# Hybrid decoder trunk on one core: activation sums of the down projection by accumulating transfers, two quadruples of weight blocks at a time, and an order of instructions set by other constants

## The chip, the cores and the metric

One of the eight cores of one Trainium2 chip runs the whole program in one launch. The metric is the device time of one execution in microseconds (us). Work is spread over the engines TensorE (PE, matrix products, with its weight loads PEld), VectorE (DVE), ScalarE (ACT), GpSimd (POOL) and SyncE (SP, which issues most transfers). Each engine takes its own instructions strictly in the order in which the program put them down, and waits on semaphores for those of other engines.

## The reference

A prompt of 1024 tokens and 8 samples of 8 tokens (1088 tokens together) go through one layer of width 1024. The part that the change is mostly about is the feed-forward part, with `D_FF = 2816`:

```python
x = x + mix @ lw['w_out']                       # mixer: attention, state space, pooling
hn2 = _rmsnorm(x, lw['norm2_g'])
up = hn2 @ lw['w_up']                           # 1024 -> 2 * 2816
up_c, conv_state = _causal_dwconv(up, conv_prefix, lw['conv_w'], lw['conv_b'])
a, g = jnp.split(up_c, 2, axis=-1)
x = x + (jax.nn.silu(g) * a) @ lw['w_down']     # 2816 -> 1024
y = _rmsnorm(x, norm_f_g)
```

Everything is float32; the mixer also returns keys, values and states.

## The kernel before

**Layout.** Features lie on the 128 partitions, tokens along the free dimension. A feature tile is [128, 1088]; `HT` = 544 is half of the tokens, `QT` = 272 a quarter. Each float32 product is made of three products of parts: an operand x is split into hi = round(x) (ACT cast to fp32r) and lo = x − hi (a TENSOR_TENSOR on DVE or POOL), and hi·hi, lo·hi, hi·lo are accumulated in PSUM.

**Order of the work.** `Driver` (line 185) steps Python generators by priority while the large products are put down; `Model` (line 36) keeps an estimate of when each engine is free, and a generator yields the estimated time at which its next step can run. So the order of instructions on each engine is fixed when the program is built, by the model's constants. Every engine call goes through one wrapper, so nearly every row of the profile bears line 156 (`L156`); instructions are told apart by the names of their tiles. `light(d)` (line 1607) gives a TENSOR_TENSOR to POOL if the model has POOL `d` us ahead of DVE, else to DVE; `parts` (line 1611) makes hi and lo, `sums` (line 1620) adds or subtracts two tiles.

**Mixer** (`phase_ab`, line 1224). The in-projection comes first, in `dense_group`s of 24 matmuls (`dps<-A,whl`). Beside it POOL computes the parameters of the state space part (`ssm_params`, line 476), ending with `ssm_cneg`, and `ssm_tables` (line 587) makes its tables; its six DVE operations `s_pn`, `X` read `ssm_pwp` and `ssm_cneg`. `bcast` (line 319) spreads 1/RMS over the partitions by a matmul of a broadcast column with the identity (`nbc`).

**Feed-forward, up** (`phase_c`, line 1625). Four feature tiles are made densely; while they run, DVE, POOL and ACT prepare the sums of the activations (`X<-X,X`, `T<-X,T`, `A<-X,A`, 128x544). Then 20 pairs f = 2 to 21 follow by `wino` (line 1575), Winograd's form of Strassen's scheme: seven products (op 0 to 6) of 24 matmuls of 272 columns on blocks of half the features and half the tokens, with PSUM tiles `wX`, `wY`, `wW`. Each result tile passes `conv` (line 1653; `cv<-raw`, 128x1104) and `gate` (line 1674; `th`), and each gated tile f goes to DRAM as `hs[f]`.

**Feed-forward, down.** Five blocks j of four feature tiles times four products mp give 20 products q = 4j + mp, each again seven ops of 12 matmuls (`wX<-hop,whl` and so on).
- Activations, per j: `hb` (line 1798) loads four tiles `hst<-hs`, makes the sums t1 to t4 (`tsums`: eight `hst<-hst` 128x544) and splits seven operands into `hop` (two halves of 544 each).
- Weights, per q: `draw` is loaded, `dsum` and `dw` (line 1856) make four sums of 128x256 (`wraw<-draw`, `draw<-...`) and seven splits `whl<-draw` / `whl<-wraw` of 128x256.
- Results: 14 additions `X<-wX,X` (`wY`, `wW`) of 128x272 from PSUM into the X tiles, on DVE.

A PSUM tile of a product comes from pools of 2, 5 and 1 banks (`bank`, line 1600) and is added to X piece by piece. The last pair of feature tiles is taken densely (`dn<-hl,whl`), followed by the norm (`final`, line 2039).

Of the kernel before, what the change touches and what calls it, by code (L numbers as in the profile page):

```python
# [12 lines left out]
P = 128  # L13
# [22 lines left out]
class Model:  # L36
    """Estimates when each instruction will run; the order in which the independent parts of the kernel
    are put down goes by it."""
    LAT = 0.13
    OWN = {"pe": 0.0, "dve": 0.1}  # L40

    def __init__(self):
        self.free = {}
        self.mem = {}
        self.ring = {}
        self.dma = 0.0
        self.tiled = False

# [9 lines left out]
    def ready(self, *aps, eng=None):  # L58
        """When the last writes to aps are done, as seen by an engine."""
# [26 lines left out]

    def note(self, eng, fn, args, kw):
# [9 lines left out]
        if fn == "dma_start":  # L97
            size = out.partition_size() * out.free_size() * 4
            self.free[eng] = start + (1.04 if eng == "pool" else 0.3)
            self.dma = max(self.dma, start + 1.4) + size / 360e3  # L100
            fin = self.dma + 1.7
        else:
            if eng == "pe":
                n = args[2].free_size()
                np_ = out.partition_size()
                if fn == "transpose":
                    c, np_ = 0.109, P
                elif args[1].dtype == F32R:
                    c = 0.0034 + n / 2400.0
                else:  # L110
                    c = 0.005 + max(4 * n / 2400.0, 0.213 * max(np_, 32) / 128.0)
                if np_ < P:
                    # column tiles run beside the first
# [3 lines left out]
                else:  # L117
                    c += 0.09 if self.tiled else 0.0
                    self.tiled = False
            elif eng == "dve":  # L120
# [8 lines left out]
            elif eng == "act":  # L129
                c = (0.07 if fn == "copy" else 0.12) + 0.83e-3 * n + (0.18 if len(outs) > 1 else 0.0)  # L130
            elif fn == "memset":
                c = 0.04 + 0.83e-3 * n
            else:
                c = 0.15 + (2.0e-3 if fn == "tensor_tensor" else 3.35e-3) * n
# [50 lines left out]
class Driver:  # L185
    """Steps the generators of the parts that run beside the large products.  A generator yields when
    its next step can run: a time, a condition, or None for at once."""
# [24 lines left out]
    def pick(self, t):  # L212
        """The generator to step: by priority among those ready at t, else the next to be ready."""
# [26 lines left out]
class Body:  # L240
# [8 lines left out]
    def acq(self, n):  # L249
        """Waits for n PSUM banks of the common ring."""  # L250
# [6 lines left out]
    def act(self, c, q, k):  # L257
        """The high (q = 0) or low part of feature tile k of the activations, token chunk c."""
# [9 lines left out]
    def rsqrt(self, x, n, width, pool=False):  # L268
        """x: [n, width] SBUF, overwritten; gives 1/sqrt(x).  pool: on Pool, else on DVE."""
# [49 lines left out]
    def bcast(self, c, y, bc=None):  # L319
        """y [tokens of a tile, tile] of chunk c as [128, tokens], the same on every partition."""  # L320
# [3 lines left out]
        for ti, (a, w) in enumerate(self.tok_tiles(c)):  # L324
            last = CH[c][1] == 320 and ti == 2
# [5 lines left out]
    def w_open(self, src, n, alloc=None):  # L331
        """src(i): DRAM AP [128, 4, 128] of half tile i; n: number of halves."""
# [40 lines left out]
    def w_split(self, upto):  # L373
        """Starts the splits of the product's halves before upto."""
# [6 lines left out]
    def dense_group(self, m, c, out_fn, last=True, pool=None):  # L381
        """One (feature tile, token chunk) of a product with K = 1024; last: the tile's last chunk."""
# [5 lines left out]
        for k in range(KD):  # L388
# [36 lines left out]
    def put_rms(self, c, y, own=False):  # L425
        """1 / RMS of chunk c to its place, the same on every partition."""
# [1783 lines left out]
```

## Time and profile before

| what | value |
|---|---|
| median of 3 runs | 1364.13 us |
| fastest and slowest run | 1362.97 and 1364.42 us |
| profiled execution, span from first to last instruction | 1362.6 us |
| median of the runs less this span | 1.5 us |
| mean granted clock of TensorE over the span | 0.970 |
| PE, DVE, POOL, ACT busy | 1272.4, 1031.8, 566.7, 539.4 us |

The span is that of one execution. The profile does not list its device time apart; what lies around the span (start and end of the launch) is taken as the 1.5 us between it and the median.
A row gives the start or a count, the busy time, engine, operation and tiles as output<-inputs. In square brackets stands how long the engine had been idle and the instruction that released it. [...]

### The profile page before, as it was taken

To read this page: it belongs to the slowest core of one execution; us is meant where nothing else is said; L and a number is where in the kernel's file an instruction comes from. 1 tells how busy PE (TensorE), PEld (TensorE's weight loads), DVE (VectorE), ACT (ScalarE), POOL (GpSimd) and SP (SyncE) were. 2 spreads that over 40 slices of the span, in tenths; PEclk is the share of its full clock that TensorE was granted. 3 is DMA by queue.
4 is the path that set the end of the run, shared out by engine and by line. 5 is a ranking of instruction groups with operands and counts; after the bars stand their busy time and mean duration, and the time that the engine had idled before them with its cause. 6 is when DMAs were issued, how large, how long until landed. Compare 5 with 4: busy or idle time off the path is not lost.

```text
span 1362.6 us, 26926 instructions
## 1 busy us (share of the span) xinstructions
PE 1272.4 (93%) x10466; PEld 1182.9 (87%) x10466; DVE 1031.8 (76%) x1990; ACT 539.4 (40%) x1127; POOL 566.7 (42%) x914
## 2 busy tenths in 40 slices
PE   7699899999999899978999999999999788888997
PEld 7697787777767899977999999999999688888997
DVE  5536765564378932897888888898889989999866
ACT  6222333333245422443545445455454333333333
POOL 7860430210012422593233232332335978768624
PEclk9899999999999999988999999999999889999997
DMA  9221212578874345202231221212212513222213
GB/s 339 87 81 33 68 40 83 183 240 289 281 246 149 83 138 157 65 24 102 106 112 55 88 82 62 95 65 79 95 49 99 186 56 113 97 68 91 81 44 132
DMA packets 80319, 154.84 MB, mean 114 GB/s; under 512 B 9856, under 2 KB 43136, under 8 KB 80192
## 3 DMA queue, kind: packets, MB, share of 16 engines
q1 hardware_dynamic: 78960, 149.68, 33.1%
q10 hardware_dynamic: 1152, 3.04, 0.6%
q8 instruction: 82, 1.34, 0.4%
q14 instruction: 45, 0.37, 0.1%
q0 software_dynamic: 80, 0.41, 0.1%
HBM read 124.04 MB, written 28.47 MB: 112 GB/s over the span
## 4 chain that ended last, share of the span: by engine, by line
PE 68%; DVE 18%; POOL 7%; issue 4%; DMA 1%; ACT 1%; POOLq 0%; DVEq 0%; SPq 0%; ACTq 0%
PE wX L156 23%; PE dps L156 15%; PE wY L156 11%; PE wW L156 5%; DVE X L156 5%; DVE whl L156 3%; POOL ssm_small L156 3%; DVE hop L156 2%; PE pv L156 2%; PE dn L156 2%; PE S L156 2%; DVE P L156 1%; PE yps L156 1%; PE od L156 1%; PE Sp L156 1%
## 5 line engine op out<-in xcount | busy, mean ns | idle before, releaser
L156 PE MATMUL dps<-A,whl 128*128 128x384 f32 (+1 forms) x1896 | 370.3, 344 | 29.7 <-DVE k L156 11.9
L156 PEld LDWEIGHTS dps<-A,whl 128*128 128x128 f32 x1896 | 319.9, 194 | 51.0 <-issue 14.9
L156 PE MATMUL wX<-T,whl 128*128 128x272 f32 x1440 | 193.0, 290 | 4.8 <-DVE whl L156 3.7
L156 PEld LDWEIGHTS wX<-T,whl 128*128 128x128 f32 x1440 | 186.1, 190 | 5.6 <-DVE whl L156 4.1
L156 PE MATMUL wX<-hop,whl 128*128 128x272 f32 x960 | 141.8, 300 | 27.1 <-DVE X L156 21.8
L156 PEld LDWEIGHTS wX<-hop,whl 128*128 128x128 f32 x960 | 130.8, 196 | 32.8 <-issue 12.1
L156 DVE SCALAR_TENSOR_TENSOR cv<-raw,vec,cv 128x1104 f32<-128x1104 f32 x88 | 126.0, 1431 | 12.2 <-ACT cv L156 10.8
L156 POOL TENSOR_TENSOR th<-th,cv 128x64 f32<-128x64 f32 (+1 forms) x40 | 79.8, 2013 | 131.2 <-DVE th L156 127.4
L156 PE MATMUL wY<-A,whl 128*128 128x272 f32 x960 | 127.6, 288 | 0.9 <-DVE whl L156 0.9
L156 PEld LDWEIGHTS wY<-A,whl 128*128 128x128 f32 x960 | 123.3, 188 | 1.1 <-DVE whl L156 1.1
L156 ACT CAST whl<-uraw 128x512 fp32r<-128x512 f32 x120 | 74.8, 623 | 81.0 <-PE wX L156 44.2
L156 ACT CAST whl<-draw 128x256 fp32r<-128x256 f32 (+1 forms) x122 | 47.8, 415 | 143.4 <-POOL draw L156 33.3
L156 POOL COPY cvo<-raw 128x2 f32<-128x2 f32 x88 | 27.6, 343 | 167.2 <-DVE raw L156 154.9
L156 ACT CAST whl<-wraw 128x512 fp32r<-128x512 f32 (+1 forms) x92 | 52.3, 570 | 112.4 <-PE dps L156 63.7
L156 DVE TENSOR_TENSOR whl<-uraw,whl 128x512 fp32r<-128x512 f32 x120 | 87.2, 727 | 12.5 <-ACT whl L156 9.9
L156 DVE TENSOR_TENSOR whl<-wraw,whl 128x512 fp32r<-128x512 f32 (+1 forms) x90 | 67.0, 745 | 31.2 <-ACT whl L156 31.2
L156 DVE TENSOR_TENSOR X<-wX,X 128x272 f32<-128x272 f32 x160 | 66.6, 431 | 14.3 <-PE wX L156 14.0
L156 PE MATMUL wY<-hop,whl 128*128 128x272 f32 x480 | 69.1, 293 | 1.0 <-DVE whl L156 1.0
L156 DVE TENSOR_TENSOR uraw<-uraw 128x512 f32<-128x512 f32 x40 | 69.2, 1729 | 0.7
L156 PEld LDWEIGHTS wY<-hop,whl 128*128 128x128 f32 x480 | 64.6, 193 | 1.6 <-DVE whl L156 1.6
L156 ACT ACTIVATE P<-P,sm 128x128 f32<-128x128 f32 (+7 forms) x64 | 35.7, 558 | 74.0 <-DVE sm L156 74.0
L156 PE MATMUL wW<-A,whl 128*128 128x272 f32 x480 | 63.2, 288 | 0.0
(271 smaller groups left out, 2336.1 us busy)
## 6 DMA issues: line engine op xcount, KB each, us to landing
K<-in_ck_dram SPq DMA_DIRECT2D x40, 512.0 KB, 6.3
V<-in_cv_dram SPq DMA_DIRECT2D x80, 256.0 KB, 4.4
uraw<-in_w_up_dram SPq DMA_DIRECT2D x40, 512.0 KB, 4.0
hs<-th SPq DMA_DIRECT2D x22, 544.0 KB, 2.7
hst<-hs SPq DMA_DIRECT2D x22, 544.0 KB, 5.3
draw<-in_w_down_dram SPq DMA_DIRECT2D x20, 512.0 KB, 3.5
wraw<-in_w_in_dram SPq DMA_DIRECT2D x28, 256.0 KB, 3.1
X<-xs SPq DMA_DIRECT2D x8, 544.0 KB, 4.4
```

Of the source, the lines that this page charges most:

```text
L156: return f(*args, **kw)
```

## The change

**Activations of the down projection.** `gate` stores its result with signs into a DRAM array per block (`hj[j]`, four blocks of two half tiles each) where before it stored whole tiles. The sums t1 to t4 are no longer computed by POOL or DVE: `chain` loads a block by SP and adds further blocks to it in SBUF with an accumulating transfer (`accum_op`) issued from POOL, 20 in all. The operand is split in the whole (128x1088) by ACT and DVE. Two chains run beside each other for each j, each in one buffer, each step waiting for the split of the step before. For j = 1 the second buffer is `T10`, apart from the gate's buffer `th`. The blocks' signs are such that sums suffice; the results of ops 1, 2 and 4 are subtracted from X, and op 3's weights are negated.

**Weights.** Two products q are handled as one pair p, so that sums and low parts are 512 wide (11 on DVE per p) instead of 256; none is on POOL. In the first pairs, where two tiles hold the draws, they are still 256 wide.

**Results.** PSUM is given anew for the down projection (`pq`, eight banks as two tags of two tiles of two banks), a product's two halves lie in one tile, and one addition of 544 follows where there were two of 272.

**Order.** `Model` gets other constants and a rule that DVE and POOL operations with two SBUF inputs exclude each other; `light` chooses POOL only if it is 2 us ahead; `parts` puts the low part always on DVE. The conv and gate of f = 21 (the last pair) come only after the first pair of weights. In the mixer, `ssm_tables` yields until `ssm_cneg` is ready, and `bcast` uses a transpose.

Counts of instructions that the order shows:

| | before | after |
|---|---|---|
| DVE, POOL, ACT instructions | 1992, 919, 1056 | 1913, 733, 987 |
| `hst<-hst` sums on POOL and DVE | 37 and 3 | none |
| accumulating transfers on POOL's queue | 0 | 20 |
| `hop` low parts | 70 of 544, 47 on DVE | 35 of 1088, all on DVE |
| weight sums and low parts of the 20 products on POOL | 118 | 0 |
| additions into X in the down projection | 280 of 272 | 140 of 544 |

The core of the diff:

```diff
-        yield None
+        yield self.M.ready(self.pwp, self.cneg)
...
-            nc.tensor.matmul(bc[:, a + (64 if last else 0):a + 128], y[:, ti:ti + 1].to_broadcast([P, 128]),
-                             self.ident[:, 64:128] if last else self.ident[:, :], start=True, stop=True)
+            nc.tensor.transpose(bc[:, a:a + 128], y[:, ti:ti + 1].to_broadcast([P, 128]), self.ident)
...
-        return self.nc.gpsimd if self.M.free.get("pool", 0.0) + d < self.M.free.get("dve", 0.0) else self.nc.vector
+        return self.nc.gpsimd if max(d, 2.0) < 9.0 and self.M.free.get("pool", 0.0) + 2.0 < self.M.free.get("dve", 0.0) else self.nc.vector
...
-            self.light(d).tensor_tensor(l, a, h.bitcast(F32), ALU.subtract)
+            yield max(self.M.ready(h), self.M.free["dve"] - 0.3 - late)
+            self.nc.vector.tensor_tensor(l, a, h.bitcast(F32), ALU.subtract)
...
-            yield lambda: n["ga"[m % 2]] >= m // 2
+            yield lambda: n["ga"[m % 2]] >= m // 2 and (m < 42 or n["dw"] >= 0)
...
-            nc.sync.dma_start(self.hs[f], th)
+            if f < 20:
+                b = f % 4 // 2 * 2
+                nc.sync.dma_start(self.hj[f // 4][:, b:b + 2, f % 2], th.rearrange("p (h t) -> p h t", h=2))
+            else:
+                nc.sync.dma_start(self.hs[f], th)
...
+        def chain(j, t, steps):
+            for pos, op, blk, add in steps:
+                yield max(M.avail(t, "dma"), M.ready(self.hj[j]))
+                if add:
+                    yield M.free["pool"] - 1.0
+                    g.dma_start(out=t, in_=self.hj[j][:, blk].rearrange("p k t -> p (k t)"), accum_op=ALU.add)
+                else:
+                    nc.sync.dma_start(t, self.hj[j][:, blk].rearrange("p k t -> p (k t)"))
+                if op is None:
+                    continue
+                yield M.ready(t)
...
+                hi, lo = [ring(j, 2 * pos + q, [P, 2, HT], F32R, "hop") for q in range(2)]
+                yield from self.parts([hi.rearrange("p k t -> p (k t)")], [lo.rearrange("p k t -> p (k t)")], [t], 9, 0 if j else 99)
...
+                    st = [cp.tile([P, NTOK], F32, tag="rms", name="hst", bufs=1),
+                          fp.tile([P, NTOK], F32, tag="T10" if j == 1 else "th", name="hst", bufs=1)]
...
+                D.add(chain(j, st[0], ((1, None, 0, False), (1, 4, 1, True), (2, 5, 3, True), (6, 3, 2, True))), "hb", 0.4)
+                D.add(chain(j, st[1], ((0, 0, 0, False), (3, 2, 3, False), (4, 6, 1, True), (5, 1, 2, False))), "hb", 0.3)
...
+        pq = self.psum_pool("pq", 2)
+        for p in range(10):
+            ps = {}
+            for op in (0, 4, 5, 2, 6, 1, 3):
...
+                    x = self.X[m][:, HT * h:HT * h + HT].rearrange("p (c t) -> p c t", c=2)
+                    v.tensor_tensor(x, x, o[:, :, :QT], ALU.subtract if op in (1, 2, 4) else ALU.add)
```

DVE in the mixer, before, from the low parts ahead of the state space tables on (`s_pn`, `X_92`: the tables; `k_671`: the key tile out of PSUM; `whl<-wraw,whl`: the low part of a weight):

```order
L156 TENSOR_TENSOR s_pn<-ssm_pwp,bc_in 128x512
L156 TENSOR_TENSOR X_92<-ssm_pwp,ssm_cneg 128x512
L156 TENSOR_TENSOR s_pn<-s_pn,X_92 128x512
L156 TENSOR_TENSOR s_pn<-ssm_pwp,ssm_cneg 128x512
L156 TENSOR_TENSOR X_92<-ssm_pwp,bc_in 128x512
L156 TENSOR_TENSOR whl<-wraw,whl 128x512
L156 TENSOR_TENSOR k_671<-dps,rms 128x384 x2
```

and in the changed kernel at the same place:

```order
L188 TENSOR_TENSOR whl<-wraw,whl 128x512
L188 TENSOR_TENSOR k_671<-dps,rms 128x384
L188 TENSOR_TENSOR s_pn<-ssm_pwp,bc_in 128x512
L188 TENSOR_TENSOR X_92<-ssm_pwp,ssm_cneg 128x512
L188 TENSOR_TENSOR s_pn<-s_pn,X_92 128x512
```

One weight's low part and the first key chunk now stand ahead of the tables; two key chunks stay behind them.

DVE in the middle of the down projection, before:

```order
L156 TENSOR_TENSOR X_11918<-wX,X_11918 128x272 x2
L156 TENSOR_TENSOR draw<-draw 128x256
L156 TENSOR_TENSOR hop<-hst,hop 128x544 x2
L156 TENSOR_TENSOR X_11920<-wY,X_11920 128x272 x2
L156 TENSOR_TENSOR X_11918<-wX,X_11918 128x272
L156 TENSOR_TENSOR whl<-draw,whl 128x256
```

and in the changed kernel:

```order
L188 TENSOR_TENSOR X_11602<-X_11602,wW 128x544
L188 TENSOR_TENSOR draw<-wraw,draw 128x2x256
L188 TENSOR_TENSOR hop<-hst,hop 128x1088
L188 TENSOR_TENSOR X_11604<-X_11604,wW 128x544
L188 TENSOR_TENSOR hop<-hst,hop 128x1088
L188 TENSOR_TENSOR X_11357<-X_11357,wX 128x544
L188 TENSOR_TENSOR whl<-wraw,whl 128x2x256
```

All pieces are twice as long, `hop` among them, and all of this work is on DVE. Nothing but transfers stands on POOL's queue in that stretch (`hj_104` to `hj_108` are the DRAM blocks j = 0 to 4):

```order
L188 DMA hst<-hj_105 128x1088 x3
L188 DMA hst<-hj_106 128x1088 x4
L188 DMA hst<-hj_107 128x1088 x4
L188 DMA hst<-hj_108 128x1088 x4
L188 DMA out_conv_dram<-cvo 128x792
L188 TENSOR_TENSOR wraw<-sqs 128x384
```

Before, this place held the 37 sums, 23 low parts of `hop` and the 118 weight operations.

DVE at the start of the feed-forward part, before (`X<-X,X` and `T<-X,T`: activation sums; the two `whl` rows: low parts for the dense tiles):

```order
L156 TENSOR_TENSOR X_88<-X_88 128x544
L156 TENSOR_TENSOR X_85<-X_89,X_85 128x544
L156 TENSOR_TENSOR whl<-wraw,whl 128x512
L156 TENSOR_TENSOR X_88<-X_92,X_88 128x544
L156 TENSOR_TENSOR X_87<-X_91,X_87 128x544
```

and in the changed kernel:

```order
L188 TENSOR_TENSOR X_86<-X_86 128x544
L188 TENSOR_TENSOR X_87<-X_87 128x544
L188 TENSOR_TENSOR X_88<-X_88 128x544
L188 TENSOR_TENSOR X_86<-X_90,X_86 128x544
L188 TENSOR_TENSOR X_87<-X_91,X_87 128x544
L188 TENSOR_TENSOR X_88<-X_92,X_88 128x544
L188 TENSOR_TENSOR X_89<-X_89,X_85 128x544
L188 TENSOR_TENSOR whl<-wraw,whl 128x512
```

Seven activation sums stand on DVE ahead of the first of these `whl` rows where there were two, and of 18 such sums that POOL had in this part, 14 are now DVE's.

## Rows read from the trace of the kernel before

**Rows 1.** The page's head, and busy time of each engine over the span.

```profile
span 1362.6 us, 26926 instructions
PE 1272.4 (93%) x10466; PEld 1182.9 (87%) x10466; DVE 1031.8 (76%) x1990; ACT 539.4 (40%) x1127; POOL 566.7 (42%) x914
```

**Rows 2.** Stretches: us, busy PE, PEld, DVE, ACT, POOL (count), clock, DMA share, GB/s.

```profile
50.00:69.00 19.00, 7.05 (x41) 6.73 (x39) 6.43 (x11) 0.00 (x0) 17.17 (x62) 0.79 0.28 87
...
573.00:655.00 82.00, 68.16 (x417) 66.76 (x416) 71.38 (x77) 34.98 (x68) 49.06 (x49) 0.90 0.20 70
655.00:1033.60 378.60, 378.60 (x3020) 378.60 (x3020) 332.53 (x450) 185.95 (x341) 114.00 (x180) 1.00 0.24 81
1033.60:1058.00 24.40, 21.86 (x170) 21.21 (x169) 24.30 (x27) 12.23 (x24) 16.84 (x13) 1.00 0.29 102
1058.00:1293.00 235.00, 206.92 (x1502) 200.36 (x1501) 218.03 (x396) 86.49 (x197) 183.89 (x168) 0.94 0.28 97
1293.00:1315.70 22.70, 22.70 (x182) 22.70 (x181) 16.79 (x37) 6.58 (x14) 8.36 (x12) 1.00 0.21 66
```

**Rows 3.** The waits of PE: tile, releaser: total us, times, longest.

```profile
PE wX L156 <- DVE X L156: 21.8, 15, 4.0
```

**Rows 4.** Timeline, 62 to 79 us, of the early stall.

```profile
63.43 0.69 DVE L156 TENSOR_TENSOR X<-ssm_pwp,ssm_cneg 128x512 f32<-128x512 f32 x1 [12.50 <-POOL ssm_cneg L156]
...
68.94 9.60 PE L156 MATMUL dps<-A,whl 128*128 128x320 f32 x42 [11.95 <-DVE k L156]
```

**Rows 5.** Timeline of PE from 548 to 646 us: a broadcast, dense groups, and stalls.

```profile
548.71 0.83 PE L156 MATMUL nbc<-ident,rs_y 128*128 128x128 f32 x6
...
573.34 17.46 PE L156 MATMUL dps<-A,whl 128*128 128x384 f32 x106
597.91 12.79 PE L156 MATMUL dps<-A,whl 128*128 128x384 f32 x60 [7.11 <-DVE whl L156]
...
616.66 11.48 PE L156 MATMUL dps<-A,whl 128*128 128x384 f32 x59 [3.00 <-DVE whl L156]
...
637.70 4.69 PE L156 MATMUL wX<-T,whl 128*128 128x272 f32 x23 [2.90 <-DVE whl L156]
642.22 3.19 PE L156 MATMUL wY<-A,whl 128*128 128x272 f32 x24
```

**Rows 6.** Timeline of POOL and DVE from 599 to 603 us.

```profile
599.68 1.83 POOL L156 TENSOR_TENSOR T<-X,T 128x544 fp32r<-128x544 f32 x1
...
602.59 0.71 DVE L156 TENSOR_TENSOR T<-X,T 128x544 fp32r<-128x544 f32 x1
```

**Rows 7.** Groups by form, 1037 to 1315 us: count | busy us, mean ns | idle before.

```profile
L156 DVE TENSOR_TENSOR X<-wX,X 128x272 f32<-128x272 f32 x158 | 65.8, 431 | 13.7 <-PE wX L156 13.4
L156 POOL TENSOR_TENSOR hst<-hst 128x544 f32<-128x544 f32 x37 | 60.8, 1661 | 3.9 <-DVE hop L156 3.3 <-DVE hst L156 0.7
L156 DVE TENSOR_TENSOR hop<-hst,hop 128x544 fp32r<-128x544 f32 x47 | 58.3, 1260 | 0.0
...
L156 ACT CAST hop<-hst 128x544 fp32r<-128x544 f32 x70 | 42.7, 644 | 31.2 <-POOL hst L156 20.4 <-DVE hst L156 10.8
```

**Rows 8.** Timeline of DVE from 1166 to 1168 us.

```profile
1166.39 0.71 DVE L156 TENSOR_TENSOR hop<-hst,hop 128x544 fp32r<-128x544 f32 x1
1167.02 0.43 DVE L156 TENSOR_TENSOR X<-wX,X 128x272 f32<-128x272 f32 x1
1167.37 0.42 DVE L156 TENSOR_TENSOR X<-wW,X 128x272 f32<-128x272 f32 x1
```

**Rows 9.** View of the tile whl on DVE: duration ns min/median/max, 512 wide.

```profile
L156 DVE TENSOR_TENSOR whl<-uraw,whl x120: 674/688/1835, 625.7 to 1051.1; 128x512 fp32r<-128x512 f32 x120
```

**Rows 10.** View of the tile hst: DVE's one low part 1088 wide, and its transfers' landing.

```profile
L156 DVE TENSOR_TENSOR hl<-hst,hl x1: 1274/1274/1274, 1279.9 to 1279.9; 128x1088 fp32r<-128x1088 f32 x1
...
DMA to landing us min/median/max: 3.4/5.3/8.0
```

**Rows 11.** View of the DMA issues: POOL's one transfer, KB and us to landing.

```profile
out_conv_dram<-cvo POOLq DMA_DIRECT2D x1, 396.0 KB, 5.8
```

More of the change, by code (lines that the diff above doesn't have):

```diff
@@ L47, in __init__, with clear @@
         self.tiled = False
+        self.port = {"dve": [], "pool": []}
+        self.win, self.act, self.slow = 0, 0.0, True
+    def clear(self, eng, t):
+        other = self.port["pool" if eng == "dve" else "dve"]
+        for a, b in reversed(other[-40:]):
+            if a <= t < b:
+                return self.clear(eng, b)
+        return t
     def seg(self, ap):
@@ L85, in alloc, with clock, two @@
         self.mem[name] = [t, {}, {}]
+    WIN = 4.096 / 1.2
+    def clock(self, t, c):
+        w = int(t / self.WIN)
+        while self.win < w:
+            self.slow = self.act < 0.42 * self.WIN
+            self.win, self.act = self.win + 1, 0.0
+        self.act += c
+        return 2 * c if self.slow else c
+    def two(self, args, kw):
+        x = [a for a in list(args[1:]) + [kw.get("in0"), kw.get("in1")] if hasattr(a, "bitcast") and a.free_size() > 1]
+        return all(a.space != bass.MemoryType.PSUM for a in x)
     def note(self, eng, fn, args, kw):
@@ L119, in note @@
                     self.tiled = False
+                c = self.clock(start, c)
             elif eng == "dve":
@@ L133, in note @@
             else:
-                c = 0.15 + (2.0e-3 if fn == "tensor_tensor" else 3.35e-3) * n
+                c = 0.13 + (2.6e-3 if fn == "tensor_tensor" else 3.35e-3) * n
+            if eng == "pool" and fn != "memset" or eng == "dve" and self.two(args, kw):
+                start = self.clear(eng, start)
+                self.port[eng].append((start, start + c))
             fin = start + c
@@ L1203, in run @@
             self.xs = [dram.tile([P, NTOK], F32, name="xs%d" % k) for k in range(8)]
-            self.hs = [dram.tile([P, NTOK], F32, name="hs%d" % f) for f in range(NFF)]
+            self.hj = [dram.tile([P, 4, 2, HT], F32, name="hj%d" % j) for j in range(5)]
+            self.hs = {f: dram.tile([P, NTOK], F32, name="hs%d" % f) for f in (20, 21)}
             self.wraw = self.wp.tile([P, 3, 4, 128], F32, name="wraw")
@@ L1897, in dw @@
-            for q in (20, 21):
-                yield lambda: n["down"] >= 4
-                r = draw.pop(q)
-                hi, lo = [ring(1, 2 * (q - 18) + z, [P, 4, 2, 128], F32R, "whl") for z in range(2)]
-                yield from self.parts([hi], [lo], [r])
-                dops[q] = (hi, lo)
-        n["dw"] = n["ds"] = n["s1"] = -1
-        def dsum():
-            for q in range(20):
-                yield lambda: q in draw and n["s1"] >= q - 2
-                a11, a12, a21, a22 = [draw[q][:, z] for z in range(4)]
-                yield M.ready(draw[q])
-                yield from self.sums(0, (s1s[q % 2], a21, a22, ALU.add), (a21, a11, a21, ALU.subtract))
-                n["ds"] = q
+            D.add(dsums(), "dsums", 0.6)
@@ L1913, in dw_1 @@
+            yield lambda: n["down"] >= 4
+            rs, qs, at = draw.pop(10)
+            for q in range(2):
+                hi, lo = [ring(1, 2 * (q + 2) + z, [P, 4, 2, 128], F32R, "whl") for z in range(2)]
+                yield from self.parts([hi], [lo], [rs[0][:, q]])
+                dops[20 + q] = (hi, lo)
+        n["dw"] = n["dw5"] = n["ds"] = -1
         def dw_1():
-            yield lambda: n["up"] == NFF or (n["up"] == NFF - 1 and n["pos"] >= 4)
+            yield lambda: n["up"] == NFF
@@ L1990, in out @@
                     if c == 1:
-                        fc[2 * f] = D.add(conv(2 * f), "conv", 3 if f < 21 else 2)
+                        fc[2 * f] = D.add(conv(2 * f), "conv", 3 if f < 20 else 4)
                 else:
@@ L1995, in out @@
                     if c == 1:
-                        fc[2 * f + 1] = D.add(conv(2 * f + 1), "conv", 3 if f < 21 else 2)
-                        fg[f] = D.add(gate(f), "gate", 1 if f < 20 else 2)
+                        fc[2 * f + 1] = D.add(conv(2 * f + 1), "conv", 3 if f < 20 else 4)
+                        fg[f] = D.add(gate(f), "gate", 1 if f < 20 else 4)
             def done(op):
@@ L2036, in phase_c @@
+        self.pt = self.psum_pool("pe", 8)
         g.dma_start(self.o["conv"], cvo)
@@ L2078, in phase_c @@
             ss = []
-            acc = fp.tile([P, 384], F32, tag="raw", name="acc", bufs=2)
+            acc = self.wr[0].rearrange("p a m -> p (a m)")[:, :384] if c % 2 else wr[:, 512:896]
             for m in range(8):
```

278 lines of the change are left out of this document (143 added, 135 removed).

## The prediction

> **What bounds the kernel now.** Start with the page's head and busy shares [rows 1]: TensorE is busy 1272.4 of 1362.6 us, so 90 us are left idle, and part of the busy time runs at a lowered clock. The question is where. The table of stretches [rows 2] answers it: from 655 to 1033.6 us (the up projection) PE is busy all the time at clock 1.00, 3020 matmuls in 378.6 us, 0.1254 us each. Nothing that another engine saves there can shorten the span. Three stretches are different: 50 to 69 us (PE busy 7 of 19), 573 to 655 us (68 of 82, clock 0.90), and the down projection from 1058 to 1293 us (207 of 235, clock 0.94). In the last 22.7 us of the down projection, where the weights are ahead, PE is full again: 182 matmuls, 0.125 us each.
>
> For the down projection, count from the first product of f = 21 to the first `dn`: 24.4 + 235.0 + 22.7 = 282.1 us [rows 2]. PE alone needs (168 + 20 x 84) x 0.1254 = 231.7 us. So 50 us are lost, the largest sum in the program. The waits of PE name the end of it: PE waits 15 times, 21.8 us together, for DVE's addition into X [rows 3]. DVE is busy 218 of 235 us there [rows 2], but not with work at full speed: its low parts of 544 take a mean of 1.260 us [rows 7], and the same form 0.71 us when alone [rows 8]. POOL, 184 us busy in the same stretch [rows 2], runs operations with two SBUF inputs, and where both engines do, they take turns: a sum of this size takes POOL 1.83 us and DVE, once POOL is done, 0.71 us [rows 6]. So DVE is late because of POOL, the bank is free late, PE stops, its clock falls.
>
> **The change, part by part.** The sum is made against the profiled execution, 1362.6 us, with 1.5 us around it, which gives the median, 1364.1.
>
> *Down projection, DVE.* POOL's 37 sums (60.8 us [rows 7]) and its low parts vanish, and nothing in this stretch competes with DVE. DVE's own price is read from starts, not durations: 0.63 us from a 544 to the next start, 0.35 us for a 272 [rows 8]: 0.07 us plus 1.03 ns an element. That gives 0.60 us for 512 and 1.19 us for 1088, where single rows show 0.688 [rows 9] and 1.274 [rows 10]. One pair p now costs 14 x 0.63 + 11 x 0.60 + 3.5 x 1.19 = 19.6 us of DVE (I use 20, with a little for small rows between). PE needs 168 x 0.1254 = 21.1 us. So PE is the bound in the middle six pairs and the last two, which lack some `hop`.
>
> The start is not covered: conv and gate of f = 21 are put behind the first weights, and there the pieces are still 256 wide. From the start of f = 21 through the second pair DVE has 28 additions (17.6), 44 pieces of 256 (15.0), 11 of 512 (6.6), 13 `hop` (15.5), eight conv passes of 1104 (9.7), the gates (4.6) and small ones (3): 72 us, against 3 x 21.1 = 63.3 of PE. So DVE is the bound there, by 9 us. Sum: 72 + 8 x 21.1 = 241. In-order waits come on top: DVE is as full as before (20 of 21.1 us, against 218 of 235), and that cost 28 us of idle PE [rows 2]. But an addition had some 1.5 us (one product of 12 matmuls) before its bank was wanted, and now has three of them. I take 8 of 28: 249 us. Ends: 239, nothing lost and a third of the 9 saved; 262, half of the old waits kept and the start late by 7 more. **Gain 33 us (20 to 43).**
>
> *Adding transfers.* No row shows a transfer that adds. The nearest: the same 544 KB loaded plainly, 5.3 us median and 3.4 to 8.0 [rows 10], and POOL's one transfer, 396 KB, 5.8 us [rows 11]. From below, 5.3; from above, twice the longest, 16 (read, add and write back). I take 7, close to the rows that exist. One chain has for each j a load, three adds of L us and three splits between: cast 2 x 0.644 less one start [rows 7], low part 1.27 [rows 10], and 0.5 of waits, 2.9 us. So 5.3 + 3L + 3 x 2.9 = 14 + 3L, and two pairs of PE are 42.1: the transfer is hidden up to L = 9.4. At 7 it costs nothing; that cover gone, each us costs three per j. The queue that carries it, POOL's, has nothing else in this stretch, so nothing stands behind its waits but the next adds.
>
> *Casts on ACT.* Same elements in half as many pieces; ACT is busy 86 of 235 us [rows 2]: nothing.
>
> *Start of the feed-forward part.* PE waits 7.11, 3.00 and 2.90 us for a low part [rows 5] (and 0.8 in two small ones), and runs slow after each: 60 matmuls in 12.79 us where 106 took 17.46 (0.165 each, 2.9 lost), 59 in 11.48 (1.8 lost), 23 in 4.69 against 24 in 3.19 (1.6 lost). Together 20 us. 14 of POOL's 18 sums become DVE's: 14 x 1.83 = 25.6 us of taking turns [rows 6] become 14 x 0.64 = 9. But DVE, in order, now has seven sums ahead of the first `whl`, so the 7.1 us wait stays; the later low parts stand some 6 us earlier, and those two waits and their slow matmuls mostly go. **Gain 8 (3 to 18).**
>
> *Early stall.* DVE sat 12.5 us behind `ssm_cneg`, with the key tile's evictions queued behind it, and PE 11.95 us behind those [rows 4]. Now one key chunk and one low part go ahead of the tables. That frees one bank: PE has 24 more matmuls, 24 x 9.60 / 42 = 5.5 us, before it stops for the second chunk, still behind the tables. POOL's own end does not move. **Gain 5 (0 to 10).**
>
> *Broadcasts.* 18 of six passes, 0.59 us each to the next start [rows 5], become 18 of three: at most half, 18 x 0.3 = 5. I take **2 (0 to 4)**. The rest of the mixer's order, and the last dense pair: 0, either way by 4.
>
> Sum: 33 + 8 + 5 + 2 = 48; 1364.1 - 48 = **1316 us**.
>
> **The rivals.** *A. DVE's operations don't overlap in time.* Then a pair costs 14 x 0.71 + 11 x 0.688 + 3.5 x 1.274 = 22.0 us, over PE's 21.1, in six pairs (5 more), and the first stretch grows by 120 x 0.07 = 8. The down projection takes 259, the gain is 23 + 15: **1326**. Against it: the addition at 1167.02 starts 0.63 us after the 544 piece that lasts 0.71 [rows 8]. For it: not every pair of pieces is ready back to back.
> [...]
>
> *B. The adds land later than the order assumes.* DVE takes its row in order, and a `hop` whose operand is not there holds the additions behind it, for which PE waits. If each of the 16 adds for j = 1 to 4 is 2 us late, 32 us of DVE stop; the pair's spare us (21.1 - 20) over eight pairs takes 9, and some overlap: 18 net. **1334**. For it: 5.3 varies up to 8.0 [rows 10].
>
> *C. Early gains don't come.* Waits in the mixer and at the start of the feed-forward part move on to the next late row (PE behind the second key chunk, DVE's longer queue ahead of `whl`), and the change does there nothing that it could: 1364 - 33 = **1331**. For it: total DVE work grows there, and POOL's end stays.
>
> *D. Slower: the adding transfer sets the pace.* The chain binds above L = 9.4; each us beyond costs 3 us in each of the four blocks j = 1 to 4, 12 us. The other gains are used up at L = 9.4 + 48/12 = 13.4. At L = 15, near the upper bound: 1316 + 12 x 5.6 = **1383**. For it: no row shows such a transfer, DVE is busy nearly all the time beside it, and a plain one reaches 8.0 [rows 10]. Against it: POOL's transfer landed in 5.8 us with DVE at work [rows 11].
> [...]
>
> **How the numbers follow.** Forecast 0.54, A 0.15, B 0.13, C 0.11, D 0.05, and 0.02 that losses eat all. 1316 is that of the likeliest. Its own range is 1299 to 1330 (all gains at their low ends give 1341, all at their high ends 1289). To hold A to C as well, with their own spread, the range reaches from 1296 to 1340. A measurement can tell about 0.2%, 2.7 us, from no change: faster 0.93 (all but D and the 0.02), same 0.02, slower 0.05.
>
> **What would show it.** Right: from the first product of f = 21 to the first `dn` 245 to 255 us, PE's wait for the addition into X under 10 us, 512-wide low parts in the down projection at 0.69 us and hardly ever over 1, adds landing in 6 to 8 us, `hop` not waited for by PE. In 573 to 655, two of the three waits gone. Wrong: additions into X waiting behind `hop` with `hop` waiting for a transfer (B, D); a median add over 9.4 us (D); DVE rows in the down projection starting only at the end of the row before (A).

## The result and the profile after

Median 1334.49 us over 4 runs (1332.78 to 1337.15), against 1364.01 of the kernel before: ratio 0.9784, 95% interval 0.9771 to 0.9798, faster by 2.2%. Forecast were 1316, range 1296 to 1340. The profiled execution took 1334.44 us, its span is 1332.3.

First the page's head and the busy times.

```profile
span 1332.3 us, 26297 instructions
PE 1258.9 (94%) x10412; PEld 1169.6 (88%) x10412; DVE 965.4 (72%) x1911; ACT 527.6 (40%) x1058; POOL 339.8 (26%) x728
```

POOL lost 227 us and DVE 66, yet the span lost 30 [rows 1]. Where, the stretches tell: early stall, end of the mixer, start of the feed-forward part, up projection, first two pairs of the down projection, the rest of it. Columns are those of [rows 2]; the clock is TensorE's granted one, a mean over the stretch, and the traces of both kernels record it as 1.00 or 0.50 and as nothing else.

```profile
50.00:69.00 19.00, 12.98 (x74) 12.24 (x72) 9.89 (x17) 1.61 (x3) 17.19 (x58) 0.90 0.38 117
440.00:490.00 50.00, 39.44 (x189) 35.87 (x188) 38.15 (x101) 15.20 (x37) 15.91 (x20) 0.80 0.24 52
581.50:625.40 43.90, 40.58 (x240) 39.97 (x239) 40.53 (x55) 21.97 (x43) 22.71 (x25) 0.97 0.13 43
625.40:1038.80 413.40, 404.24 (x3194) 402.34 (x3193) 330.50 (x502) 199.06 (x385) 113.15 (x189) 1.00 0.28 84
1060.20:1111.80 51.60, 43.88 (x314) 42.55 (x313) 47.83 (x81) 20.89 (x38) 6.70 (x9) 0.93 0.85 243
1111.80:1263.20 151.40, 150.61 (x1190) 149.68 (x1189) 141.94 (x204) 55.99 (x75) 10.94 (x13) 1.00 0.56 144
```

In the last row PE is full at clock 1.00 and POOL has nothing but its transfers, where before PE was 207 of 235 and POOL 184 [rows 2]. Read from PE's timeline, by four marks (last broadcast of the mixer, first product of f = 2, first product of f = 21, first `dn`), all in us:

| piece | before | after | difference | forecast |
|---|---|---|---|---|
| mixer, to its last broadcast | 572.6 | 580.9 | +8.3 | -7 |
| start of the feed-forward part | 55.3 | 44.4 | -10.9 | -8 |
| up projection, f = 2 to f = 21 | 405.7 | 413.4 | +7.7 | 0 |
| f = 21 and down projection | 282.1 | 247.1 | -35.0 | -33 |
| last dense pair and norm | 46.8 | 46.4 | -0.4 | 0 |

The two largest terms came as forecast, and 16 us were given back where the forecast had a gain of 7 and nothing. PE's waits show where the up projection lost its part.

```profile
PE wX L188 <- DVE whl L188: 11.1, 9, 2.2
...
PE dps L188 <- DVE k L188: 5.3, 1, 5.3
PE dps L188 <- DVE whl L188: 4.8, 4, 2.6
PE pps L188 <- DVE X L188: 4.5, 2, 3.4
...
PE wW L188 <- DVE X L188: 0.2, 1, 0.2
```

PE's wait for the addition into X is gone (0.2 us, before 21.8 [rows 3]). New is the first row, 9 waits for a low part. Seven of them lie 43.4 us apart, from 685 to 945 us, in the up projection, where PE had no wait between 655 and 1033 us before. The timeline at the first of them:

```profile
682.58 0.44 DVE L188 TENSOR_TENSOR raw<-wW,st 128x272 f32<-128x272 f32 x1 [3.41 <-PE wW L188]
682.93 1.54 DVE L188 SCALAR_TENSOR_TENSOR th<-th,cv 128x64 f32<-128x64 f32 x3
...
684.40 0.68 DVE L188 TENSOR_TENSOR whl<-uraw,whl 128x512 fp32r<-128x512 f32 x1
...
685.13 0.64 PE L188 MATMUL wX<-T,whl 128*128 128x272 f32 x3 [0.99 <-DVE whl L188]
```

DVE stands idle for 3.41 us with the low part behind it in its queue. In front is an addition that waits for PE's own product, then three gate pieces; the low part, whose high part was there, comes last and PE waits for it.

The down projection's own rows, DVE's starts and the transfers' landing (issue to landing, median):

```profile
1143.07 0.71 DVE L188 TENSOR_TENSOR X<-X,wY 128x544 f32<-128x544 f32 x1
1143.70 1.29 DVE L188 TENSOR_TENSOR hop<-hst,hop 128x1088 fp32r<-128x1088 f32 x1
1144.90 0.69 DVE L188 TENSOR_TENSOR draw<-draw 128x512 f32<-128x512 f32 x1
1145.51 0.71 DVE L188 TENSOR_TENSOR X<-X,wX 128x544 f32<-128x544 f32 x1
```

```profile
hst<-hj SPq DMA_DIRECT2D x20, 544.0 KB, 5.0
hst<-hj POOLq DMA_DIRECT2D x20, 544.0 KB, 6.1
```

From start to start an addition takes 0.63 us, a `hop` 1.20, a weight operation 0.61: each starts some 0.08 us before the one ahead has ended, as [rows 8] had it. An adding transfer takes 6.1 us, 1.1 more than a plain one beside it.

### The profile page after: what moved, and what is told of

It reads as the page before. It is cut to its first block, busy times and chain, and to the rows that moved or that the text cites. A ratio compares the mean times of both kernels' runs of the same rounds, so it can differ in the third digit from the quotient of the medians.

```text
span 1332.3 us, 26297 instructions
## 1 busy us (share of the span) xinstructions
PE 1258.9 (94%) x10412; PEld 1169.6 (88%) x10412; DVE 965.4 (72%) x1911; ACT 527.6 (40%) x1058; POOL 339.8 (26%) x728
## 4 chain that ended last, share of the span: by engine, by line
PE 72%; DVE 12%; POOL 7%; issue 4%; DMA 3%; ACT 1%; SPq 0%; POOLq 0%; DVEq 0%; ACTq 0%
PE wX L188 25%; PE dps L188 16%; PE wY L188 13%; PE wW L188 5%; POOL ssm_small L188 3%; DVE X L188 2%; PE pv L188 2%; PE S L188 2%; PE od L188 2%; PE Sp L188 1%; DVE whl L188 1%; PE tp L188 1%; PE yps L188 1%; DVE th L188 1%; POOL X L188 1%
## 5 line engine op out<-in xcount | busy, mean ns | idle before, releaser
L188 PE MATMUL dps<-A,whl 128*128 128x384 f32 (+1 forms) x1896 | 375.2, 346 | 21.2 <-ACT whl L188 6.7
L188 DVE SCALAR_TENSOR_TENSOR cv<-raw,vec,cv 128x1104 f32<-128x1104 f32 x88 | 119.3, 1366 | 22.2 <-ACT cv L188 21.9
L188 PE MATMUL wX<-hop,whl 128*128 128x272 f32 x960 | 127.1, 289 | 3.0 <-DVE whl L188 2.2
L188 PEld LDWEIGHTS wX<-hop,whl 128*128 128x128 f32 x960 | 123.3, 189 | 3.8 <-DVE whl L188 2.6
L188 ACT CAST whl<-wraw 128x512 fp32r<-128x512 f32 (+1 forms) x96 | 56.8, 599 | 156.4 <-PE dps L188 67.6
L188 DVE TENSOR_TENSOR whl<-uraw,whl 128x512 fp32r<-128x512 f32 x120 | 106.4, 893 | 7.0 <-ACT whl L188 7.0
L188 POOL TENSOR_TENSOR th<-th,cv 128x64 f32<-128x64 f32 (+1 forms) x36 | 55.6, 1546 | 116.4 <-DVE th L188 105.1
L188 DVE TENSOR_TENSOR whl<-wraw,whl 128x512 fp32r<-128x512 f32 (+1 forms) x96 | 68.6, 719 | 21.2 <-ACT whl L188 20.5
L188 PE MATMUL wX<-A,whl 128*128 128x272 f32 x480 | 63.2, 288 | 0.0
L188 DVE TENSOR_TENSOR X<-X,wX 128x544 f32<-128x544 f32 x80 | 57.0, 720 | 6.5 <-PE wX L188 6.0
L188 PEld LDWEIGHTS wW<-A,whl 128*128 128x128 f32 x480 | 61.3, 189 | 0.0
```

What stands on the lines that cost most here:

```text
L188: return f(*args, **kw)
```

## The experiments

Theories: **T**, the down projection gained as worked out (DVE's start-to-start sum, a hidden chain of transfers), and the time given back was lost by the order of rows on DVE, in the up projection and at the end of the mixer. Rivals: slower transfers, more DVE work or run-to-run differences gave it back; or the transfers, the wide pieces or the banks alone made the gain. Times of a stretch are from one profiled execution; medians and ratios are against the kernel before, run beside each.

### Order in the up projection

```diff
                 c = (0.09 + 0.83e-3 * n if fn == "copy" else 0.1 + 1.0e-3 * n) + (0.18 if len(outs) > 1 else 0.0)
+                if self.old:
+                    c = (0.07 if fn == "copy" else 0.12) + 0.83e-3 * n + (0.18 if len(outs) > 1 else 0.0)
...
+            M.old = 3 <= f < 20
             n["up"], n["pos"] = f, -1
```

> The planner's cost of ACT operations goes back to the one of the kernel before for f = 3 to 19, so only the order from the up projection on differs. Theory (in every second f a low part stands on DVE behind an addition that waits for PE's wW and three gate pieces): the first product of f = 2 to that of f = 21 goes from 413.4 us to 405 to 406, the whole to about 1326. Rival (the up projection is slower because all low parts are on DVE and the gate is in three pieces): it stays at 412 or more, 1334.

(Later texts call this the second run.) 1318.79 us, ratio 0.9676 (0.9650 to 0.9702). The up projection takes 404.7 us, 8.7 less, and the seven waits are gone with the same instructions, three-piece gate and DVE low parts included:

```profile
621.00:1025.70 404.70, 402.48 (x3194) 402.06 (x3193) 320.53 (x503) 198.88 (x385) 122.65 (x189) 1.00 0.29 86
```

So the loss in the up projection is the order's, shown. The total fell by 15.7 us, more than the 8 expected; profile against profile, the stretch from f = 21 to `dn` was 242.4 (-4.7), and the mixer, whose rows stand in the same order, ended 4.6 us earlier in this execution.

### The end of the mixer

In the changed kernel DVE waits 4.81 us there for a residual load, with the pooling branch behind it:

```profile
457.81 0.56 DVE L188 TENSOR_TENSOR X<-dps,k 128x384 f32<-128x384 f32 x1 [4.81 <-DMA k<-in_xT_dram]
```

```diff
+            if (m, c) == (0, 0):
+                D.until(lambda: self.pool_n >= 6)
             xo = self.X[m][:, t0:t0 + n]
```

> The edit puts the pooling branch's vector operations ahead of the first residual addition X<-dps,k of the output projection, nothing else; the planner then also shifts rows behind it. Theory (two places in DVE's order cost the time): DVE's 4.8 us wait for the transfer k<-in_xT goes, the dense restart that stood at 581.5 us comes some 8 us earlier, near the 573.3 of the kernel before; as the low part in the up projection now also stands ahead of the rows that wait for PE, the seven stalls of 1 us go too, 8 us more: about 1318 us. Rival (slower transfers and more DVE work, not the order): the wait moves to another row, under 3 us in each place, 1330 or more.

1331.21 us, ratio 0.9761 (0.9737 to 0.9785). That wait fell to 0.8 us, and nothing came of it: the last broadcast stood at 581.0, PE was busy 38.6 of the 50 us from 440 (39.4 before the edit). The wait moved to other rows, as the rival had it. The seven waits in the up projection stayed, against the expectation. In this profile the down projection was 4.2 us shorter (242.9) and the up projection 2.1, and the start of the feed-forward part 2.8 longer; that is how the 3 us come about.

```diff
+            self.M.old = True
             self.phase_ab()
+            self.M.old = False
             self.phase_c()
...
```

The lines left out give `Model`, while `old` is set, its former costs for PE, ACT and POOL and take away the rule that DVE and POOL exclude each other.

> The planner's costs in the mixer are those of the kernel before (broadcast by transpose and the wait of the tables stay), and its cost of ACT operations for f = 3 to 19 too, as in the second run. Theory (the mixer's 8 us loss comes from its other order): the last broadcast before the feed-forward part comes at 570 to 574 us instead of 576 to 581, the whole 1309 to 1314. Rival (the loss comes from the broadcast and the tables, or from transfers): it stays at 576 to 581, 1317 to 1322.

1318.58 us, ratio 0.9656 (0.9628 to 0.9683), the rival's value. Last broadcast at 578.5. Here the early stall nearly vanished, and it can be followed how the lead was lost:

```profile
50.00:69.00 19.00, 16.08 (x94) 15.44 (x92) 8.65 (x13) 1.24 (x2) 17.25 (x59) 1.00 0.45 146
69.00:440.00 371.00, 355.64 (x3822) 280.15 (x3822) 225.36 (x651) 123.00 (x308) 72.82 (x196) 0.97 0.47 152
440.00:490.00 50.00, 41.63 (x247) 37.17 (x240) 39.65 (x103) 14.36 (x34) 14.22 (x15) 0.83 0.26 64
```

The kernel before, last two stretches:

```profile
69.00:440.00 371.00, 361.64 (x3859) 287.80 (x3860) 223.65 (x658) 122.84 (x303) 76.53 (x196) 0.98 0.48 154
440.00:490.00 50.00, 45.72 (x320) 41.77 (x318) 41.63 (x98) 18.84 (x42) 18.43 (x20) 1.00 0.37 110
```

PE did 9 us more work in the first stretch than before [rows 2], 6 us less from there to 440 us and 4 us less from 440 to 490, where its granted clock was also lower (0.83 against 1.00). The order is not quite that of the kernel before: broadcast, tables and a constant of 0.02 us between dependent operations of one engine are still the new ones.

The next takes the whole mixer of the kernel before, with the old broadcast, tables and constants, in front of the rest:

```diff
-        yield self.M.ready(self.pwp, self.cneg)
+        yield None
...
-            nc.tensor.transpose(bc[:, a:a + 128], y[:, ti:ti + 1].to_broadcast([P, 128]), self.ident)
+            nc.tensor.matmul(bc[:, a + (64 if last else 0):a + 128], y[:, ti:ti + 1].to_broadcast([P, 128]),
+                             self.ident[:, 64:128] if last else self.ident[:, :], start=True, stop=True)
...
+            self.M.old, self.M.OWN = True, {"pe": 0.0, "dve": 0.1}
...
```

> The mixer is that of the kernel before in every part (broadcast by matmul, tables without the wait, all planner's costs), the rest is the change with the up projection's order of the second run. Theory (the mixer's 8 us loss is the change's): the last broadcast before the feed-forward part at 571 to 575 us, the whole 1308 to 1314. Rival (the mixer ends with a chain whose end varies from run to run, and the change there neither gains nor loses): 576 to 582, the whole 1314 to 1321.

1320.26 us, ratio 0.9674 (0.9634 to 0.9713), but four runs spread from 1312.31 to 1324.74, and the profiled one was the fastest: its last broadcast stands at 565.8, 7 us ahead of the same program's in the kernel before. PE was busy 46.6 us from 440 to 490, as before:

```profile
440.00:490.00 50.00, 46.58 (x304) 44.18 (x304) 36.23 (x91) 18.52 (x42) 16.81 (x18) 1.00 0.34 107
```

In the medians the mixers cannot be told apart (1318.6 to 1320.3), as the rival had it; the profiled execution, mark and time, is on the theory's side. By the mark alone, the two profiles with the old broadcast, tables and order have 565.8 and 572.6, the twelve with the new broadcast and tables 576.3 to 583.5 (ten of them with the very same order of rows). No trace shows where the three slower executions lost their time. So whether the new mixer loses time or only gains none stays open. By stretches the new one gains at 50 us and loses from 440 to 490. Which rows cost that is left open too: the one wait that was named was not it.

### The sums without adding transfers

```diff
-                    g.dma_start(out=t, in_=self.hj[j][:, blk].rearrange("p k t -> p (k t)"), accum_op=ALU.add)
+                    for k in range(2):
+                        s = fp.tile([P, HT], F32, tag="stg%d" % (steps[0][1] is None), name="stg", bufs=1)
+                        nc.sync.dma_start(s, self.hj[j][:, blk, k])
+                        yield max(M.ready(s), M.free["pool"] - 1.0)
+                        a = t[:, HT * k:HT * k + HT]
+                        g.tensor_tensor(a, a, s, ALU.add)
```

> The 20 accumulating transfers become plain loads by SP and two POOL additions of 544 each; all else of the change stays. Theory (the gain in the down projection is that POOL no longer takes turns with DVE): 32 to 40 sums of about 1.7 us hold up DVE; from the first product of f = 21 to the first dn 265 to 280 us instead of 247, the whole 1352 to 1367. Rival (the gain comes from wider pieces and from the longer slack of the PSUM banks): under 255, the whole under 1343.

1369.12 us, ratio 1.0041 (1.0026 to 1.0056); f = 21 to `dn` 283.3. The number is the theory's, its reason isn't: POOL spent 59 us on sums but waited 111 us for the staging transfers, and DVE's `hop` took 1.50 us against 1.29. With one half-block tile a chain has loads and sums strictly in turn:

```profile
L188 POOL TENSOR_TENSOR hst<-hst,stg 128x544 f32<-128x544 f32 x38 | 58.7, 1548 | 183.5 <-DMA stg<-hj 111.2 <-DVE hop L188 46.5 <-DVE wraw L188 25.8
L188 DVE TENSOR_TENSOR hop<-hst,hop 128x1088 fp32r<-128x1088 f32 x35 | 52.1, 1501 | 0.9 <-ACT hop L188 0.9
```

How much of the stretch is the taking of turns, this run cannot say. How much it is on DVE, the traces do: measured against the shortest row of the same tiles and form, DVE's rows from f = 21 to `dn` ran 67 us longer in sum in the kernel before, 2 in the changed one and 25 here.

> The 20 accumulating transfers become plain loads and two DVE additions of 544 each. Theory (DVE's start-to-start cost against PE's 21.1 us a pair): 4 x 0.64 = 2.6 us more DVE a pair, 22.6 against 21.1, so eight pairs give 1.5 each and the first stretch 5: down projection 260 to 267 instead of 247, the whole 1347 to 1354. Rival (DVE has more room than that, its waits hide it): under 252, the whole under 1340.

The same with `v.tensor_tensor`, placed by DVE's time in the plan: 1364.27 us, ratio 1.0010 (0.9994 to 1.0026); 273.7, slower than either expected. DVE was busy 252 us of the stretch in this run and in the one before: 38 sums took it 27 us here, and the same sums on POOL lengthened its rows by 25 there.

```diff
-                        nc.sync.dma_start(s, self.hj[j][:, blk, k])
+                        g.dma_start(s, self.hj[j][:, blk, k])
```

> As the run before with the sums on DVE, but the plain loads into the half-block staging tile are issued by POOL, so that SP's queue (weights' draws) never stands behind a wait for that tile. Theory (two costs, DVE's 2.6 us a pair and SP standing up to 7.75 us behind the staging tile): the second goes, first product of f = 21 to first dn 258 to 266 us instead of 273.7, the whole 1344 to 1352. Rival (DVE's extra work and its order alone): within 3 us of 273.7.

1354.12 us, ratio 0.9915 (0.9881 to 0.9949); 275.0, the rival's: SP's queue was not the cause. The 10 us by which the total is less came in the up projection (404.4 against 416.6), where this edit touches no instruction: the plan came out another way, and one of the seven waits is left. In this run the `wW` products of every second pair, from the third on, come 50.4, 50.6 and 51.0 us apart. By 14 + 3L that would be L = 12.2: two half loads of 3.1 us and two sums are 7.6 of it, the rest would be waits between them, which no row here was followed for. That speaks for the chain of one block as what set the pace; the next run tries it.

A whole tile for the staging of the longer chains takes the strict turns away (and five of the 20 sums stay transfers, so it is not the tile alone that differs):

```diff
+                    if steps[0][1] is None:
+                        s = fp.tile([P, NTOK], F32, tag="stg", name="stg", bufs=1)
+                        nc.sync.dma_start(s, self.hj[j][:, blk].rearrange("p k t -> p (k t)"))
+                        for a in (0, HT):
+                            yield max(M.ready(s), M.free["dve"] - 0.3)
+                            v.tensor_tensor(t[:, a:a + HT], t[:, a:a + HT], s[:, a:a + HT], ALU.add)
+                    else:
...
```

> The 15 accumulating transfers of the longer chains become plain loads of whole blocks into a tile of their own, and two DVE additions of 544 each; the five of the shorter chains stay accumulating transfers. A block's load and its sums take about 6 + 1.4 us, so by 14 + 3L the chain (36 us) stays hidden under 42. Theory (the chain with a half-block tile, L about 12, made the two runs before slow; with a whole tile only DVE's 1.9 us a pair is left, 21.9 against 21.1): first product of f = 21 to first dn 253 to 261 us, the whole 1339 to 1347. Rival (DVE's extra work with its in-order waits is what costs 27 us): 268 or more, 1354 and up.

1347.12 us, ratio 0.9876 (0.9857 to 0.9894); 254.8, as the theory had it, 7.7 more than with the transfers. DVE is now the full engine (150.3 of 152 us):

```profile
1119.00:1271.00 152.00, 145.53 (x1144) 143.98 (x1143) 150.29 (x218) 56.22 (x74) 3.16 (x4) 1.00 0.46 147
```

### The adding transfer twice

```diff
                     g.dma_start(out=t, in_=self.hj[j][:, blk].rearrange("p k t -> p (k t)"), accum_op=ALU.add)
+                    g.dma_start(out=t, in_=self.hj[j][:, blk].rearrange("p k t -> p (k t)"), accum_op=ALU.add)
```

> Each accumulating transfer is issued twice, one behind the other, so a block is added twice (the sums are other ones; the work is that of the change plus 20 transfers). Theory (chain of a load, three adds and splits per j, 14 + 3L us against 42.1 of PE, hidden up to L = 9.4): L goes from 6.1 to about 12.5, each of four blocks gets 9 us longer, the stretch of 247 us becomes 275 to 290, the whole 1362 to 1377. Rival (the chain has more room than that, as a chain of one block overlaps the products of the block before): under 257 us, the whole under 1344.

1404.16 us, ratio 1.0283 (1.0251 to 1.0314); f = 21 to `dn` 316.7. The theory's side, but 27 us beyond its upper end. PE now waits five times for `hop` in `wW` (22.6 us together), and the `wW` products of every second pair lie 55.6 us and more apart, the least here:

```profile
1179.23 4.14 PE L188 MATMUL wW<-hop,whl 128*128 128x272 f32 x24
...
1234.80 1.42 PE L188 MATMUL wW<-hop,whl 128*128 128x272 f32 x10
```

The last four blocks took 55.2, 54.6, 58.3 and 57.3 us, 56.4 in the mean. By 14 + 3L that is L = 14.1, twice 6.7 (the median here) and 0.7 between. So the formula fits the four blocks (54 us more than in the changed kernel), the price I put in was 1.6 too low, and of the remaining 15 us, 13.6 fall in the first block (start of f = 21 to its first `wW`, 37.0 us before the edit, 50.6 with it), which I had left out.

### Pieces and deferral

```diff
-                    x = self.X[m][:, HT * h:HT * h + HT].rearrange("p (c t) -> p c t", c=2)
-                    v.tensor_tensor(x, x, o[:, :, :QT], ALU.subtract if op in (1, 2, 4) else ALU.add)
+                    for c in range(2):
+                        x = self.X[m][:, HT * h + QT * c:HT * h + QT * c + QT]
+                        v.tensor_tensor(x, x, o[:, c, :QT], ALU.subtract if op in (1, 2, 4) else ALU.add)
```

> The additions into X are two of 272 again instead of one of 544; the banks and all else stay. Theory (start to start 0.35 us for 272 and 0.63 for 544): 14 x 0.07 = 1 us more DVE a pair, 21 us against PE's 21.1, so little is left hidden: 2 to 8 us on the stretch of 247, 1337 to 1342. Rival (operations do not overlap, 0.43 x 2 against 0.72: 2 us a pair, 22 to 23 against 21.1): 10 us or more, 1345 and up.

1342.16 us, ratio 0.9837 (0.9801 to 0.9873); 254.0, 6.9 more: inside the theory's 2 to 8. Five of the eight pairs behind the second took 22.6 or 22.7 us, the rival's figure, the others 21.2 to 21.4; but the operations do overlap. Two additions of 272 fill 0.69 us from start to start where one of 544 took 0.63:

```profile
1142.79 0.77 DVE L188 TENSOR_TENSOR X<-X,wX 128x272 f32<-128x272 f32 x2
1143.48 0.67 DVE L188 TENSOR_TENSOR whl<-draw,whl 128x512 fp32r<-128x512 f32 x1
```

```diff
-            yield lambda: n["ga"[m % 2]] >= m // 2 and (m < 42 or n["dw"] >= 0)
+            yield lambda: n["ga"[m % 2]] >= m // 2
```

> The conv and gate of f = 21 are no longer held back until the first pair's weights are split. Theory (the held back work is what DVE can spare; without the deferral it stands ahead of the first weights): PE waits for the first down product, first product of f = 21 to first hop product 24 to 27 us instead of 21.4, and the stretch to dn 249 to 255 instead of 247. Rival (DVE has the same work either way in the first 72 us): the stretch stays within 2 us of 247.

1331.41 us, ratio 0.9762 (0.9745 to 0.9780); hop product at 21.4 us as before, `dn` after 243.0. The theory falls: the deferral buys nothing. The rival missed as well, by 2 us, and that tells how far a stretch can be trusted: seven profiles with the same additions, sums and splits there (the change, the runs on the up projection's order, on the mixer and on the deferral) took 242.4 to 247.1, DVE's rows standing in another order in each, and the change itself is the longest. Against the shortest, the 6.9 of the 272-wide run are 11.6 and the 7.7 of the whole-tile run 12.4.

> The second run's order in the up projection together with the last run's undone deferral. If the two add up: 1318.8 less 3 us, 1314 to 1318. If the deferral is worth nothing and the 4 us of the last run were the spread of one execution: 1318 to 1321.

1322.57 us, ratio 0.9684 (0.9657 to 0.9711), above both ranges: the two do not add up. Up 404.7, f = 21 to `dn` 244.0, last broadcast 581.1. The second run, 1318.8, stays the version to take.

## Why the prediction was right or wrong

- **Down projection, 33 forecast, 35.0 found.** The parts hold too. f = 21 to the end of the second pair (1038.8 to 1114.8; its last 24 matmuls stand in the row that starts at 1111.8): 72 forecast by DVE's row of work, 76.0 found, 12.7 over PE. A pair behind that: 21.1 to 21.4 us in all but one (22.6), against 21.1. Allowed for in-order waits were 8 us; 4.0 came in the first stretch and 2.3 behind it (171.1 to `dn` against 168.8). The addition into X is waited for 0.2 us.
- **The adding transfer, 7 us taken, 6.1 found** (3.6 to 9.7 with the plain ones), hidden up to 9.4. D did not occur; the doubled transfer shows that its mechanism is real. Of B there is a trace: DVE stood six times, 9.4 us together, for a `hop` whose cast had waited for a transfer, the longest 2.71 us behind the one add of 9.7, in the first pair. It cost little, not 18 us:

```profile
L188 DVE TENSOR_TENSOR hop<-hst,hop 128x1088 fp32r<-128x1088 f32 x35 | 45.0, 1290 | 9.5 <-ACT hop L188 9.4
```

- **DVE's overlap**: start to start 0.63, 0.61 and 1.20, forecast 0.63, 0.60 and 1.19. Rival A is out, here as in [rows 8]. (By its own terms its time was 249 + 5 + 8 = 262 for the down projection, not 259, and so 1329, not 1326.) With 272-wide additions, 0.06 us an addition more already shows: DVE is 94% busy beside a full PE.
- **Start of the feed-forward part, 8 forecast, 10.9 found.** PE's first wait for a low part (7.11 [rows 5]) did not stay, as I took it, but fell to 2.65.
- **The step that failed: "Early stall ... Gain 5" and "Broadcasts ... 2 (0 to 4)".** The early stall shrank as worked out (PE's wait 11.95 to 5.3 us, 5.9 us more work by 69 us), and then the lead was lost from 440 to 490 us, where PE was busy 39.4 us against 45.7, at clock 0.80 against 1.00. Counted by the matmuls left before the first of f = 2 (broadcasts apart), the changed kernel was 5.5 us ahead of the kernel before with 1000 left and 7.9 behind with 750 left: 13 us, some 6 of them idle time and the rest, as an estimate from the two clocks, slower matmuls. I had priced a local wait as if it were on the way to the end and gave the other rows of the mixer "0, either way by 4"; in this profile the mixer ended 8.3 us later. Run to run that end moves by about 7 us (565.8 and 572.6 with the old mixer, 576.3 to 583.5 with the new), and medians with either mixer agree within 2 us. So the 7 us of gain did not come, as rival C has it for the mixer; whether 8 us were lost beside that, and by which rows, stays open.
- **A term that was missing: the up projection.** I argued that nothing there could shorten the span, PE being full, and took this for "cannot lengthen" too. DVE's queue had been put in another order there, seven low parts came 1 us late, and 7.7 us were lost. The second run, in the section on the order in the up projection, shows it.

Together: 7 us of gain that didn't come and 16 lost, less 5 us that the two good terms brought beyond forecast, make the 18 between 1316 and 1334. The time lies above the forecast's own range (1299 to 1330), in the part that rivals B and C had opened, and that is partly luck: C's reason (1331) held for the mixer alone, the start of the feed-forward part gained more than forecast, B cost little, and the up projection's 7.7 us stood in no rival.

What made the 35 us is only partly taken apart: wide additions 6.9 to 11.6 of it, sums by transfer rather than by DVE 7.7 to 12.4 (15 of 20 sums). The remainder, POOL out of DVE's way and the longer slack of the banks, was not tested apart. The traces give the first its size on DVE (rows 67 us longer in sum before, 2 after), but not its worth in time, as DVE took over POOL's share of the weights and low parts; staging j = 1 in the gate's buffer was not tried.

## What to carry to other kernels

When a change touches the constants of a planner, every stretch that the planner orders is changed, also the full ones: compare the order of the queues in each, and look for a row that waits for PE in front of one for which PE waits. A wait that is removed early in a stretch counts only if what ends that stretch comes earlier. A chain of transfers needs its own sum (load, adds, splits) against the work that hides it; a staging tile that is too small can turn it into the bound. Sums handed to POOL were no relief for DVE here: 25 us of longer rows against 27 us for doing them.

## What the runs showed of the hardware

An accumulating transfer of 544 KB from DRAM into SBUF, issued by POOL, landed in 6.1 us (median of 20), against 5.0 for SP's plain loads of the same size (median of 20). DVE was busy 141.9 of the 151.4 us from 1111.8 us on, in which 12 of the 20 were issued. The issue of one took POOL 0.86 us (median):

```profile
1145.28 0.86 POOL L188 DMA_DIRECT2D hst<-hj  x1 [9.20 <-DVE hop L188]
```

The plain half loads of the two runs that add on DVE by a half-block tile, issued by POOL (first row) and by SP (second row), landed in the same time, 3.1 us:

```profile
stg<-hj POOLq DMA_DIRECT2D x40, 272.0 KB, 3.1
stg<-hj SPq DMA_DIRECT2D x40, 272.0 KB, 3.1
```

So the 1.1 us more of the adding transfer are hardly the queue's; what they are, no run shows.

DVE's operations here start some 0.08 us before the one ahead of them has ended: in the rows of the changed kernel at 1143 us, an addition lasted 0.71 us and the next operation started 0.63 us after it did, and a `hop` lasted 1.29 us and the next started 1.20 us after it did.

Where DVE and POOL both had two inputs in SBUF, they took turns, as the prediction read it. In the kernel before, DVE started a `hop` of 544 at 1163.22 us, beside one of POOL's that ended at 1164.52; DVE's lasted 1.87 us, to 0.58 us behind that end, and the next one, at 1166.39, 0.71 us [rows 8]. Of DVE's 47 such `hop`, 36 started at least 0.3 us before the end of a TENSOR_TENSOR of POOL's, and all 36 ended 0.58 us behind it. DVE's additions of 272 with one input in PSUM lasted 0.42 to 0.44 us there, all 278 of them, 206 beside an operation of POOL's.
